# Delta rule by chunks: a group's heads in two halves of the partitions, with the scan's products alternating between the halves of the array

## Chip, cores and metric

The kernel runs on one core of one Trainium2 chip. The metric is the device time of one execution in microseconds. Before the change three timed runs took 1833.44, 1835.93 and 1836.46 us, with a median of 1835.93.

## What is computed

The reference is one transformer block for 256 tokens of width 2048 in f32: modulation of the input by a vector c, a token mixer with two branches (attention in a window with sinks, and a gated delta rule), and a mixture of 32 experts of which each token uses two. The change touches the delta rule alone. It has 8 heads of dimension 128, and the 256 tokens are cut into 4 chunks of 64:

```python
def gated_delta_rule(q, k, v, g, beta):
    ...
    cum = jnp.cumsum(g, axis=-1)                  # inside each chunk
    a_mat = jnp.where(strict, beta[..., :, None] * kk * decay_incl, 0.0)
    t_mat = lax.linalg.triangular_solve(a_mat + eye, ...)
    u = t_mat @ (v * beta[..., None])
    w = t_mat @ (k * (beta * jnp.exp(cum))[..., None])
    qk = jnp.einsum('bhncd,bhnjd->bhncj', q, k) * decay_incl
    ...
    def step(state, xs):
        u_c, w_c, qk_c, qd_c, kd_c, dec_c = xs
        v_new = u_c - w_c @ state
        o_c = qd_c @ state + qk_c @ v_new
        state = dec_c[..., None, None] * state + jnp.swapaxes(kd_c, -1, -2) @ v_new
        return state, o_c
```

Ahead of it stand a causal convolution of width 4 over q, k and v and a SiLU; behind it a norm over each head and a gate.

## The kernel before

The weights stream through TensorE once. The input projection is cut into blocks of 128 output columns. A block comes as a tile of 1 MB; each half of it is split into a high and a low part (`split`, L272: a cast wh on ScalarE at L275, a difference wl on VectorE at L276), and 24 matmuls of 128x256 take a half (`mm3`, L279 to L282, into tiles named ws, wq, pp). These matmuls are called the stream here. In between, VectorE works off the modulation of the second half of the block (`ada_steps`, L211: products with w_ada at L220).

The branches are Python generators, called chains. `run` (L345) goes through the list of jobs (one job is one half of a block), and between the quarters of each job it lets the chain take steps: `per` steps a job, where a step is what the generator does up to its next `yield`, and counts 1 unless the yield gives another number. What is left of a chain after the last job is issued at once. The stages around the change are these:

- L775: `gates`, the attention and a SiLU as the chain, 1.66 steps a job, with the first 12 blocks of q, k and v as the stream;
- L777: `gdn(0)`, heads 0 to 3, 1.55 steps a job, with the second 12 blocks;
- L823: `gdn(1)`, heads 4 to 7, 0.85 steps a job, with gate and output projections;
- L840: `out_b`, which turns the outputs o back (L831) and multiplies them with the gate.

A scheduler then fixes each engine's queue when the program is built. It can pull a few stream matmuls of the next run in among the last steps of a chain. On the chip each queue runs in that order.

In `gdn` (L459) the partitions hold tokens: 128 of them, that is two chunks, c=0 in partitions 0 to 63 and c=1 in 64 to 127. A unit u = 4t + h is head h in the tokens of tile t. After norms (L484 to L502), decays (L510 to L520) and the products pk and pq (L530, L531), a solve over six levels (L555 to L573) inverts the matrix of each chunk and head. Its products (`each`, L539 to L544) are 64x64 blocks, and with c innermost they alternate between rows and columns 0 to 63 of the array and 64 to 127. Each level has a step py for t=0, one for t=1, then a step prr (with ptt) for t=0 and one for t=1.

The scan (L579 to L618) goes through the chunks ci = 0 to 3 with the state St (128 x 4 heads x 128). Chunk ci lies in one half r of the partitions, and so all four heads' products of a group use the same half:

- ks and qs (L588, L592): keys and queries times the state, 128 rows of the array and 64 columns, both followed by VectorE on 64 x 512 (L589, L590, L593);
- vn (L600): the solved matrix times the corrected values, 64 rows and 64 columns, then a copy on ScalarE (L601);
- ds (L606): keys times new values, 64 rows and 128 columns, then decay on GpSimd (L608) and addition into St on VectorE (L609, L611);
- po (L614): 64 rows and 64 columns, then addition into o (L616, L618).

All of these go to PSUM tiles from one pool of five (`pg`, L141). In `conv_todo` (L444) ScalarE writes a scaled copy of a block to its place in G0 (L452), and VectorE adds three shifted ones in place (L454).

Of the kernel before, what the change touches and what calls it, by code (L numbers as in the profile page):

```python
# [16 lines left out]
P = 128  # L17
# [49 lines left out]
def tile_block(ctx: ExitStack, tc: tile.TileContext, A: dict, out: bass.AP, dbg=None, upto=99):  # L67
# [306 lines left out]
    beta = gd.tile([P, NT, GH], F32, name="beta")  # L374
    cum = gd.tile([P, NT, GH], F32, name="cum")
    ecum = gd.tile([P, NT, GH], F32, name="ecum")
    kdw = gd.tile([P, NT, GH], F32, name="kdw")
    dec = gd.tile([P, 2 * NT, GH], F32, name="dec")

    def gates():  # L380
# [55 lines left out]
        SC.activation(kdw, kdw, AF.Exp)  # L436

# [5 lines left out]

    def conv_todo(gi):  # L444
        g0s[gi] = r2.tile([P, 16, S], F32, tag=f"X{2 - gi}", name=f"G0{gi}")

        def use(m, ps):
            mi = 12 * gi + m
            y = g0s[gi][:, m, :]
            raw = gd.tile([P, S], F32, tag="cy", name=f"cy{mi}", bufs=2)  # L450
            SC.copy(raw, ps)
            SC.activation(y, ps, AF.Copy, scale=conv[:, mi, 3:4])  # L452
            for sft in (1, 2, 3):
                V.scalar_tensor_tensor(y[:, sft:], raw[:, :S - sft], conv[:, mi, 3 - sft:4 - sft], y[:, sft:],  # L454
                                       op0=MUL, op1=ADD)

        return [(20 + 12 * gi + m, lambda ps, m=m: use(m, ps)) for m in range(12)]

    def gdn(gi):  # L459
        h0 = gi * HG  # L460
        g0 = g0s[gi]
        qk, vT = g0[:, 0:8, :], g0[:, 8:12, :]
        kd = g0[:, 12:16, :].rearrange("p h s -> p (h s)").rearrange("p (t h d) -> p t h d", t=NT, h=HG)
        g1 = r1.tile([P, 1024 + 7 * 512], F32, tag="G1", name=f"G1{gi}")
        vt = g1[:, 0:1024].rearrange("p (t h d) -> p t h d", t=NT, h=HG)
# [11 lines left out]
        nn = gd.tile([P, 2, NT, HG], F32, tag="nn", name=f"nn{gi}")  # L477
        rn = gd.tile([P, 2, NT, HG], F32, tag="rn", name=f"rn{gi}", bufs=2)
        scr = gd.tile([P, P], F32, tag="scr", name=f"scr{gi}")
        for t in range(NT):  # L480
            for j in range(2):
                p = pg(f"nt{gi}{t}{j}")
                for h in range(HG):
                    T.transpose(p[:, h * P:(h + 1) * P], qk[:, 4 * j + h, t * P:(t + 1) * P], ident)  # L484
                for h in range(HG):
                    SC.activation(scr, p[:, h * P:(h + 1) * P], AF.Square, accum_out=nn[:, j, t, h:h + 1])
                if j:
                    V.tensor_copy(kd[:, t], p.rearrange("p (h d) -> p h d", h=HG))
            yield
        SC.activation(nn, nn, AF.Sqrt, bias=epsr)  # L490
        V.reciprocal(rn, nn)
        wj = gd.tile([P, NT, HG], F32, tag="wj", name=f"wj{gi}")
        wk = gd.tile([P, NT, HG], F32, tag="wk", name=f"wk{gi}")
        V.tensor_tensor(wj, rn[:, 1], rn[:, 1], op=MUL)
        V.tensor_tensor(wj, wj, beta[:, :, h0:h0 + HG], op=MUL)
        V.tensor_tensor(wk, wj, kdw[:, :, h0:h0 + HG], op=MUL)
        for t in range(NT):
            G.tensor_tensor(kd[:, t], kd[:, t], wk[:, t, :].unsqueeze(2).to_broadcast([P, HG, P]), op=MUL)
            p = pg(f"vv{gi}{t}")
            for h in range(HG):  # L500
                T.transpose(p[:, h * P:(h + 1) * P], vT[:, h, t * P:(t + 1) * P], ident)
            V.tensor_tensor(vt[:, t], p.rearrange("p (h d) -> p h d", h=HG),  # L502
                            nn[:, 1, t, :].unsqueeze(2).to_broadcast([P, HG, P]), op=MUL)
        yield
        cg = gd.tile([P, NT, HG], F32, tag="cg", name=f"cg{gi}")
        V.tensor_copy(cg, cum[:, :, h0:h0 + HG])
        cgu = cg.rearrange("p t h -> p (t h)").unsqueeze(2).to_broadcast([P, U, 64])
        wju = wj.rearrange("p t h -> p (t h)").unsqueeze(2).to_broadcast([P, U, 64])
# [15 lines left out]
        for t in range(NT):  # L524
            for h in range(HG):
                u = t * HG + h
                for c in range(2):
                    cs = slice(t * P + 64 * c, t * P + 64 * c + 64)
                    r = slice(64 * c, 64 * c + 64)
                    T.matmul(u3(pk)[r, u, :], qk[:, 4 + h, cs], qk[:, 4 + h, cs], start=True, stop=True)  # L530
                    T.matmul(u3(pq)[r, u, :], qk[:, 4 + h, cs], qk[:, h, cs], start=True, stop=True)  # L531
# [23 lines left out]
        for l in range(6):  # L555
            for t in range(NT):
                py = pg(f"py{gi}{l}{t}")[:, :256]
                each(py, BT, (lambda u: M("id64")) if l == 0 else (lambda u: u3(Tm)[:, u, :]), t)
                V.tensor_tensor(h3(half(Y, t)), h3(py), hb(lev[:, l, :]), op=MUL)
                yield  # L560
            for t in range(NT):
                prr = pg(f"prr{gi}{l}{t}")[:, :256]
                each(prr, Y, (lambda u: M("id64")) if l == 0 else (lambda u: u3(Rm)[:, u, :]), t)
                if l == 0:
                    G.tensor_tensor(h3(half(Tm, t)), hb(M("id64")), h3(half(Y, t)), op=SUB)
                    V.tensor_tensor(h3(half(Rm, t)), hb(M("id64")), h3(prr), op=SUB)
                else:
                    if l < 5:
                        pt = pg(f"ptt{gi}{l}{t}")[:, :256]
                        each(pt, Rm, lambda u: u3(Y)[:, u, :], t)  # L570
                        V.tensor_tensor(half(Tm, t), half(Tm, t), pt, op=SUB)
                    V.tensor_tensor(half(Rm, t), half(Rm, t), prr, op=SUB)
                yield  # L573

        f = lambda ap: ap.rearrange("p (h d) -> p h d", h=HG)
        X, Vn, St = f(b5[0]), f(b5[1]), f(b5[5])
        o = gd.tile([P, NT, HG, P], F32, tag="o", name=f"o{gi}", bufs=2)
        o_t[gi] = o
        for ci in range(2 * NT):  # L579
            t, c = ci // 2, ci % 2  # L580
            r = slice(64 * c, 64 * c + 64)
            cs = slice(t * P + 64 * c, t * P + 64 * c + 64)
            eb = ecum[r, t, h0:h0 + HG].unsqueeze(2).to_broadcast([64, HG, P])
            if ci:
                p1 = f(pg(f"ks{gi}{ci}"))
                p3 = f(pg(f"qs{gi}{ci}"))
                for h in range(HG):
                    T.matmul(p1[r, h, :], qk[:, 4 + h, cs], St[:, h, :], start=True, stop=True)  # L588
                V.tensor_tensor(X[r], p1[r], eb, op=MUL)  # L589
                V.tensor_tensor(X[r], vt[r, t], X[r], op=SUB)  # L590
                for h in range(HG):
                    T.matmul(p3[r, h, :], qk[:, h, cs], St[:, h, :], start=True, stop=True)  # L592
                V.tensor_tensor(o[r, t], p3[r], eb, op=MUL)  # L593
                xs = X[r]
                yield
            else:
                xs = vt[r, t]
            p2_ = f(pg(f"vn{gi}{ci}"))
            for h in range(HG):
                T.matmul(p2_[r, h, :], u3(Rm)[r, t * HG + h, :], xs[:, h, :], start=True, stop=True)  # L600
            SC.copy(Vn[r], p2_[r])  # L601
            yield
            if ci < 2 * NT - 1:
                p4 = f(pg(f"ds{gi}{ci}"))
                for h in range(HG):
# [6 lines left out]
            p5 = f(pg(f"po{gi}{ci}"))  # L612
            for h in range(HG):
                T.matmul(p5[r, h, :], u3(qkT)[r, t * HG + h, :], Vn[r, h, :], start=True, stop=True)  # L614
            if ci:
                V.tensor_tensor(o[r, t], o[r, t], p5[r], op=ADD)  # L616
            else:
                V.tensor_copy(o[r, t], p5[r])  # L618
            yield
        ssq = gd.tile([P, NT, HG], F32, tag="ssq", name=f"ssq{gi}")  # L620
        rq = gd.tile([P, NT, HG], F32, tag="rq", name=f"rq{gi}")
        for t in range(NT):
            for h in range(HG):
                SC.activation(scr, o[:, t, h, :], AF.Square, accum_out=ssq[:, t, h:h + 1])
# [6 lines left out]
        for t in range(NT):  # L631
            G.tensor_tensor(o[:, t], o[:, t], ssq[:, t, :].unsqueeze(2).to_broadcast([P, HG, P]), op=MUL)
# [192 lines left out]
    def out_b():  # L825
        oo = r2.tile([P, 2, 8, S], F32R, tag="X1", name="oB")
        oh[1], ol[1] = oo[:, 0], oo[:, 1]
        for j in range(8):
            p = pg(f"ot{j}")
            for t in range(NT):  # L830
                T.transpose(p[:, t * P:(t + 1) * P], o_t[j // HG][:, t, j % HG, :], ident)  # L831
            V.scalar_tensor_tensor(szT[:, j, :], p[:, :S], SM("nw"), szT[:, j, :], op0=MUL, op1=MUL)
            hilo(oh[1][:, j, :], ol[1][:, j, :], szT[:, j, :])
            yield
# [694 lines left out]
```

## Time and profile before

| | us |
|---|---|
| median of three timed runs | 1835.93 |
| the profiled execution | 1836.7 |
| its span, first to last instruction | 1834.7 |
| TensorE busy in it | 1742.0 |
| VectorE busy | 906.3 |
| ScalarE busy | 516.5 |
| GpSimd busy | 42.1 |

The mean granted TensorE clock is 0.987 of full speed. In a row of the profile stand line, engine, operation, output and inputs with their shapes, the count, then busy time in us and the mean of one in ns, then the idle time of the engine ahead of it and what ended it. A shape such as 64*64 ahead of an operand is the part of the array that a matmul uses, rows by columns. PE is TensorE, PEld its weight loads, DVE VectorE, ACT ScalarE, POOL GpSimd, SP the queue that issues transfers. Ends of matmuls are modelled, so that distances are better read from start to start.

### The profile page before, as it was taken

How to read it: one execution, taken by the hardware profiler on the slowest of the kernel's cores; microseconds unless marked ns; L12 is line 12 of the kernel's file. 1: busy time of each engine (PE TensorE's matmuls, PEld its weight loads, DVE VectorE, ACT ScalarE, POOL GpSimd, SP SyncE). 2: the span in 40 equal slices, each digit the busy share in tenths (PEclk: the TensorE clock that was granted, in tenths of full speed). 3: DMA queues.
4: the chain of work that ended last, by engine and by line, in shares of the span. 5: the costliest groups of instructions: out<-in, count | busy, mean ns of one | idle time of the engine just before them, and what ended most of it. 6: DMA issues, size and time to landing. Idle time of an engine off the chain costs nothing. (4 is left out here: it accounts for less than half of the span.)

```text
span 1834.7 us, 27454 instructions
## 1 busy us (share of the span) xinstructions
PE 1742.0 (95%) x11514; PEld 1122.4 (61%) x11514; DVE 906.3 (49%) x1447; ACT 516.5 (28%) x956; POOL 42.1 (2%) x47
## 2 busy tenths in 40 slices
PE   5999999999999999998899999999999999999995
PEld 3778988898999999986444443444434444344341
DVE  3355898788878878668233222332223312232135
ACT  3333699336323444434211100111101110011101
POOL 1000000102000000000000000000000000000000
PEclk8999999999999999999999999999999999999998
DMA  8888566455877578878799999999999999999995
GB/s 356 320 320 312 211 245 225 174 207 200 300 266 269 205 284 325 345 303 354 319 383 420 420 420 421 420 421 420 421 420 420 420 421 420 420 420 421 401 422 232
DMA packets 87287, 628.58 MB, mean 343 GB/s; under 512 B 9828, under 2 KB 9828, under 8 KB 11252
## 3 DMA queue, kind: packets, MB, share of 16 engines
q1 hardware_dynamic: 86832, 626.43, 85.6%
q8 instruction: 92, 1.51, 0.3%
q10 hardware_dynamic: 328, 0.36, 0.1%
q14 instruction: 35, 0.29, 0.0%
HBM read 624.65 MB, written 2.10 MB: 342 GB/s over the span
## 5 line engine op out<-in xcount | busy, mean ns | idle before, releaser
L275 ACT CAST wh<-w 128x1024 fp32r<-128x1024 f32 x216 | 225.9, 1049 | 319.0 <-PE ws L281 114.1
L276 DVE TENSOR_TENSOR wl<-w,wh 128x1024 fp32r<-128x1024 f32 x216 | 264.8, 1226 | 81.0 <-PE mx L281 22.8
L1187 PE MATMUL pg<-w,XT 128*64 128x512 f32 x1024 | 277.9, 598 | 5.0 <-DMA w<-in_w_gu 2.8
L1187 PE MATMUL pu<-w,XT 128*64 128x512 f32 x1024 | 274.6, 592 | 0.0
L280 PE MATMUL ws<-uh,wh 128*128 128x256 f32 x896 | 261.2, 292 | 1.1 <-ACT wh L275 1.1
L282 PE MATMUL ws<-uh,wl 128*128 128x256 f32 x896 | 254.5, 284 | 4.4 <-DVE wl L276 3.9
L281 PE MATMUL ws<-ul,wh 128*128 128x256 f32 x896 | 253.7, 283 | 0.0
L1225 PE MATMUL pd<-w,hT 128*64 128x512 f32 x1016 | 234.1, 599 | 0.8 <-DVE hT L1202 0.8
L1194 DVE TENSOR_TENSOR hs<-hs,pu 128x512 f32<-128x512 f32 x16 | 11.0, 688 | 429.3 <-PE pu L1187 429.3
L280 PEld LDWEIGHTS ws<-uh,wh 128*128 128x128 f32 x896 | 169.8, 190 | 11.6 <-issue 7.5
L282 PEld LDWEIGHTS ws<-uh,wl 128*128 128x128 f32 x896 | 170.1, 190 | 8.6 <-DVE wl L276 7.1
L281 PEld LDWEIGHTS ws<-ul,wh 128*128 128x128 f32 x896 | 170.1, 190 | 0.5 <-issue 0.5
L220 DVE SCALAR_TENSOR_TENSOR acc<-w,csil,acc 128x1024 f32<-128x1024 f32 x128 | 164.3, 1300 | 10.6 <-DMA w<-in_w_ada 10.3
L1187 PEld LDWEIGHTS pu<-w,XT 128*64 128x64 f32 x1024 | 77.6, 137 | 146.2 <-issue 146.2
L1187 PEld LDWEIGHTS pg<-w,XT 128*64 128x64 f32 x1024 | 72.3, 136 | 135.5 <-issue 111.8
L1166 PEld LDWEIGHTS xg<-G,xh 128*128 128x128 f32 x1024 | 118.9, 191 | 41.2 <-issue 25.8
L1225 PEld LDWEIGHTS pd<-w,hT 128*64 128x64 f32 x1016 | 66.5, 136 | 124.0 <-issue 109.6
L1166 PE MATMUL xg<-G,xh 128*128 128x128 f32 x1024 | 130.5, 281 | 6.8 <-DVE x L1242 3.5
L1193 ACT ACTIVATE hs<-pg 128x512 f32<-128x512 f32 x16 | 9.6, 598 | 439.1 <-PE pg L1187 439.1
L370 ACT CAST dh<-pd 128x512 fp32r<-128x512 f32 x64 | 37.5, 586 | 281.3 <-DVE pd L1228 160.8
L1228 DVE SCALAR_TENSOR_TENSOR pd<-pd,wsl,g2b 128x512 f32<-128x512 f32 x64 | 48.5, 758 | 104.0 <-PE pd L1225 104.0
L280 PE MATMUL wq<-uh,wh 128*128 128x256 f32 x320 | 93.7, 296 | 5.1 <-ACT uh L176 2.7
(365 smaller groups left out, 2298.0 us busy)
## 6 DMA issues: line engine op xcount, KB each, us to landing
w<-in_w_gu SPq DMA_DIRECT2D x256, 1024.0 KB, 19.8
w<-in_w_dn SPq DMA_DIRECT2D x127, 1024.0 KB, 19.8
w<-in_w_ada SPq DMA_DIRECT2D x64, 1024.0 KB, 5.0
w<-in_w_in SPq DMA_DIRECT2D x56, 1024.0 KB, 5.0
w<-in_w_a SPq DMA_DIRECT2D x28, 1024.0 KB, 6.3
w<-in_w_kq SPq DMA_DIRECT2D x20, 1024.0 KB, 6.4
w<-in_w_pab SPq DMA_DIRECT2D x16, 1024.0 KB, 5.3
w<-in_w_out SPq DMA_DIRECT2D x16, 1024.0 KB, 6.0
```

Of the source, the lines that this page charges most:

```text
L220: V.scalar_tensor_tensor(acc[:, hc], w[:, hc], csil[:, k:k + 1], acc[:, hc], op0=MUL, op1=ADD)
L275: SC.copy(h, w)
L276: V.tensor_tensor(lo, w, h.bitcast(F32), op=SUB)
L280: T.matmul(p, a[0], b[0], start=first, stop=False)
L281: T.matmul(p, a[0], b[1], start=False, stop=False)
L282: T.matmul(p, a[1], b[0], start=False, stop=last)
L370: SC.copy(h, src)
L1166: T.matmul(p[:, k * P:(k + 1) * P], xh[t][:, (4 * kq + k) * P:(4 * kq + k + 1) * P], Gs[t].bitcast(F32), start=(t == 0), stop=(t == NT - 1))
L1187: T.matmul(dst[64 * e:64 * e + 64, :], XT[:, k, 64 * e:64 * e + 64], we[:, e * 1024 + hv * 512:e * 1024 + hv * 512 + 512], start=(k == 0), ...
L1194: V.tensor_tensor(hs, hs, pup, op=MUL)
L1225: T.matmul(pd[64 * e:64 * e + 64, :], hT[:, f, 64 * e:64 * e + 64], we[:, (2 * (f % 2) + e) * 512:(2 * (f % 2) + e + 1) * 512], start=(f = ...
L1228: V.scalar_tensor_tensor(pd, pd, ws, g2b[:, cs], op0=MUL, op1=MUL)
```

## The change

The partitions of the delta rule no longer hold two chunks of a head, but one chunk of two heads. With a = 0 or 1 for the half of the partitions and e = 0 or 1 for the place within it, head e + 2a of a group stands in half a; a unit is u = 2 ci + e. So:

- the four products of each group in the scan alternate between the halves (the list `heads`), and the VectorE and ScalarE operations behind them are on 128 x 256 instead of 64 x 512. The two halves of ds go to two PSUM tiles, and are added into St in two operations. This makes one more PSUM tile per chunk out of the same pool of five;
- in the solve, both t are issued in one step, which counts 2;
- q, k and v are stored by place, chunk, half and token (`units`). The convolution therefore builds its sum in a tile of its own (cs, two of them, by turns), and its last addition writes to G0 in four pieces of 64;
- the gates beta, cum, ecum and kdw stand in one tile, gates4. A new last step of `gates` swaps the halves with two products (sw) and copies them to gc4, by chunk and head; each `gdn` then takes four small copies from there in place of one (cg);
- `out_b` turns two heads at once: four products into a tile, instead of two.

The diff, cut to its core:

```diff
@@ gates
+        yield
+        p = pg("sw")[:, :8 * GH].rearrange("p (q h) -> p q h", h=GH)
+        gq = gates4.rearrange("p q t h -> p (q t) h")
+        for a in range(2):
+            T.matmul(p[64 * a:64 * a + 64], ident[:, 64 - 64 * a:128 - 64 * a], gq, start=True, stop=True)
+        for a in range(2):
+            r = slice(64 * a, 64 * a + 64)
+            for c, src in ((a, gq), (1 - a, p)):
+                V.tensor_copy(gc4[r, :, c], src[r].rearrange("p q (g a e) -> p q a g e", g=2, a=2)[:, :, a])
...
@@ conv_todo
+        return g0[:, 4 * j:4 * j + 4, :].rearrange("p h s -> p (h s)").rearrange("p (e c a i) -> p e c a i", e=2, c=4, a=2)
...
-            SC.activation(y, ps, AF.Copy, scale=conv[:, mi, 3:4])
-            for sft in (1, 2, 3):
-                V.scalar_tensor_tensor(y[:, sft:], raw[:, :S - sft], conv[:, mi, 3 - sft:4 - sft], y[:, sft:],
+            SC.activation(sm[:, 1:], ps[:, :S - 1], AF.Copy, scale=conv[:, mi, 2:3])
+            for sft in (2, 3):
+                V.scalar_tensor_tensor(sm[:, sft:], raw[:, :S - sft], conv[:, mi, 3 - sft:4 - sft], sm[:, sft:],
                                        op0=MUL, op1=ADD)
+            V.scalar_tensor_tensor(y, raw.rearrange("p (c i) -> p c i", c=4), conv[:, mi, 3:4],
+                                   sm.rearrange("p (c i) -> p c i", c=4), op0=MUL, op1=ADD)
...
@@ gdn, solve
                 each(py, BT, (lambda u: M("id64")) if l == 0 else (lambda u: u3(Tm)[:, u, :]), t)
                 V.tensor_tensor(h3(half(Y, t)), h3(py), hb(lev[:, l, :]), op=MUL)
-                yield
+            yield 2.0
...
-                yield
+            yield 2.0
...
@@ gdn, scan
+        heads = [(e + 2 * a, slice(64 * a, 64 * a + 64), e) for e in range(2) for a in range(2)]
...
-                for h in range(HG):
-                    T.matmul(p1[r, h, :], qk[:, 4 + h, cs], St[:, h, :], start=True, stop=True)
-                V.tensor_tensor(X[r], p1[r], eb, op=MUL)
-                V.tensor_tensor(X[r], vt[r, t], X[r], op=SUB)
+                for h, r, e in heads:
+                    T.matmul(p1[r, e, :], ks[:, e, ci, h // 2], St[:, h, :], start=True, stop=True)
+                V.tensor_tensor(X, p1, eb, op=MUL)
+                V.tensor_tensor(X, vt[:, us], X, op=SUB)
...
-            for h in range(HG):
-                T.matmul(p2_[r, h, :], u3(Rm)[r, t * HG + h, :], xs[:, h, :], start=True, stop=True)
-            SC.copy(Vn[r], p2_[r])
+            for h, r, e in heads:
+                T.matmul(p2_[r, e, :], u3(Rm)[r, 2 * ci + e, :], xs[r, e, :], start=True, stop=True)
+            SC.copy(Vn, p2_)
             yield
             if ci < 2 * NT - 1:
-                p4 = f(pg(f"ds{gi}{ci}"))
-                for h in range(HG):
-                    T.matmul(p4[:, h, :], kd[r, t, h, :], Vn[r, h, :], start=True, stop=True)
+                p4 = [f2(pg(f"ds{gi}{ci}{a}")) for a in range(2)]
+                for h, r, e in heads:
+                    T.matmul(p4[h // 2][:, e, :], kd[r, 2 * ci + e, :], Vn[r, e, :], start=True, stop=True)
                 if ci:
                     G.tensor_tensor(St, St, dec[:, ci, h0:h0 + HG].unsqueeze(2).to_broadcast([P, HG, P]), op=MUL)
-                    V.tensor_tensor(St, St, p4, op=ADD)
-                else:
-                    V.tensor_copy(St, p4)
...
+                for a in range(2):
+                    if ci:
+                        V.tensor_tensor(St[:, 2 * a:2 * a + 2], St[:, 2 * a:2 * a + 2], p4[a], op=ADD)
+                    else:
+                        V.tensor_copy(St[:, 2 * a:2 * a + 2], p4[a])
```

qs and po change as ks and vn do. The transposes and the pk and pq products keep their number and shapes, with other columns of G0.

More of the change, by code (lines that the diff above doesn't have):

```diff
@@ L371, in hilo, with by_chunk @@
         V.tensor_tensor(lo, src, h.bitcast(F32), op=SUB)
[L374 to L377, printed above, removed]
+    gates4 = gd.tile([P, 4, NT, GH], F32, name="gates4")
+    beta, cum, ecum, kdw = [gates4[:, q] for q in range(4)]
+    gc4 = gd.tile([P, 4 * NT, 2, 2, 2], F32, name="gc4")
+    def by_chunk(q, gi):
+        return gc4[:, NT * q:NT * q + NT, :, gi].rearrange("p t c e -> p (t c) e")
     dec = gd.tile([P, 2 * NT, GH], F32, name="dec")
@@ L442, in tile_block, with units @@
     o_t = [None, None]
+    def units(g0, j):
+        return g0[:, 4 * j:4 * j + 4, :].rearrange("p h s -> p (h s)").rearrange("p (e c a i) -> p e c a i", e=2, c=4, a=2)
+    cys = [gd.tile([P, S], F32, name=f"cs{j}") for j in range(2)]
+    for cy in cys:
+        G.memset(cy[:, 0:1], 0.0)
     def conv_todo(gi):
@@ L523, in gdn @@
         pq = pg(f"pq{gi}")
[L524 to L531, printed above, removed]
+        for u in range(U):
+            q_, k_ = qs[:, u % 2, u // 2], ks[:, u % 2, u // 2]
+            for a in range(2):
+                r = slice(64 * a, 64 * a + 64)
+                T.matmul(u3(pk)[r, u, :], k_[:, a], k_[:, a], start=True, stop=True)
+                T.matmul(u3(pq)[r, u, :], k_[:, a], q_[:, a], start=True, stop=True)
         yield
@@ L578, in gdn @@
         o_t[gi] = o
+        heads = [(e + 2 * a, slice(64 * a, 64 * a + 64), e) for e in range(2) for a in range(2)]
         for ci in range(2 * NT):
[L580 to L583, printed above, removed]
+            us = slice(2 * ci, 2 * ci + 2)
+            eb = eg_[:, us].unsqueeze(2).to_broadcast([P, 2, P])
             if ci:
[L585 to L589, printed above, removed]
-                V.tensor_tensor(X[r], vt[r, t], X[r], op=SUB)
[L591 to L594, printed above, removed]
+                p1 = f2(pg(f"ks{gi}{ci}"))
+                p3 = f2(pg(f"qs{gi}{ci}"))
+                for h, r, e in heads:
[3 more added lines that the diff above has]
+                for h, r, e in heads:
+                    T.matmul(p3[r, e, :], qs[:, e, ci, h // 2], St[:, h, :], start=True, stop=True)
+                V.tensor_tensor(o[:, us], p3, eb, op=MUL)
+                xs = X
@@ L612, in gdn @@
-            p5 = f(pg(f"po{gi}{ci}"))
-            for h in range(HG):
-                T.matmul(p5[r, h, :], u3(qkT)[r, t * HG + h, :], Vn[r, h, :], start=True, stop=True)
+                for a in range(2):
+                    if ci:
+                        V.tensor_tensor(St[:, 2 * a:2 * a + 2], St[:, 2 * a:2 * a + 2], p4[a], op=ADD)
+                    else:
+                        V.tensor_copy(St[:, 2 * a:2 * a + 2], p4[a])
+            p5 = f2(pg(f"po{gi}{ci}"))
+            for h, r, e in heads:
+                T.matmul(p5[r, e, :], u3(qkT)[r, 2 * ci + e, :], Vn[r, e, :], start=True, stop=True)
@@ L625, in gdn @@
+        rq = gd.tile([P, U], F32, tag="rq", name=f"rq{gi}")
+        for u in range(U):
+            SC.activation(scr, o[:, u, :], AF.Square, accum_out=ssq[:, u:u + 1])
         V.tensor_scalar(rq, rn[:, 0], 128 ** -0.5, None, op0=MUL)
```

90 lines of the change are left out of this document (49 added, 41 removed).

## Prediction

> **What bounds the kernel now.** I read the page first, then the busy time by stage, then who waited for whom on the way to the end of the delta rule, then TensorE's timeline.
>
> ```profile
> span 1834.7 us, 27454 instructions
> PE 1742.0 (95%) x11514; PEld 1122.4 (61%) x11514; DVE 906.3 (49%) x1447; ACT 516.5 (28%) x956; POOL 42.1 (2%) x47
> ```
>
> TensorE is busy for 95% of the span, but that is an average. The stages show where the change lies (columns: from and to in us, length, busy us of PE, PEld, DVE, ACT and POOL with counts, granted clock, DMA share, GB/s):
>
> ```profile
> 200.00:302.00 102.00, 95.65 (x762) 87.20 (x760) 92.40 (x167) 90.81 (x235) 0.92 (x3) 1.00 0.63 230
> 302.00:430.00 128.00, 124.02 (x1362) 112.39 (x1361) 100.50 (x145) 54.24 (x108) 13.09 (x10) 0.97 0.52 188
> 430.00:614.00 184.00, 180.97 (x1856) 170.15 (x1854) 149.91 (x176) 72.18 (x125) 17.80 (x12) 1.00 0.73 270
> 640.00:760.00 120.00, 119.47 (x995) 117.39 (x994) 96.33 (x113) 52.89 (x71) 1.81 (x1) 1.00 0.83 306
> ...
> 1000.00:1400.00 400.00, 390.82 (x1944) 167.23 (x1942) 107.67 (x214) 41.10 (x90) 0.00 (x0) 1.00 1.01 420
> ```
>
> The first row is gates and attention, the next two are gdn(0) and gdn(1). In all of them TensorE works through one queue in which projection matmuls (the stream: ws, pp) alternate with steps of the delta rule. It stands still for 4.0 of 128 us in gdn(0) and 3.0 of 184 in gdn(1), and VectorE is at 79% and 81%. So there a microsecond less of TensorE instructions is a microsecond less of time, as long as the other engines keep up. The last row is the expert stage: DMA share 1.01 at 420 GB/s. It is bound by transfers, but its loads start when the earlier stages have freed their buffers, and from 640 to 760 us TensorE is busy for 119.5 of 120 us; what is saved before 614 us therefore moves the whole expert stage forward, at one to one.
>
> Who TensorE waited for, 200 to 640 us (total, times, longest):
>
> ```profile
> PE py L544 <- DVE G L535: 5.1, 2, 4.0
> PE pa L708 <- DVE attP L699: 2.0, 1, 2.0
> ```
>
> These few waits are what a shorter queue could lengthen.
>
> **What a detour costs.** One f32 product is two passes in the trace. A group of four scan products, all on one half of the array (vn, 64*64), stands between stream matmuls like this:
>
> ```profile
> 394.01 0.28 PE L281 MATMUL ws<-ul,wh 128*128 128x256 f32 x1
> 394.13 0.28 PE L282 MATMUL ws<-uh,wl 128*128 128x256 f32 x1
> 394.33 1.08 PE L600 MATMUL vn<-G 64*64 64x128 f32 x8
> 395.35 0.39 PE L280 MATMUL ws<-uh,wh 128*128 128x256 f32 x1
> 395.57 0.28 PE L281 MATMUL ws<-ul,wh 128*128 128x256 f32 x1
> ```
>
> Stream matmuls start 0.12 us apart. From 394.13 to the second one behind the group at 395.57 are 1.44 us; two stream steps would be 0.24, so the detour costs 1.20. Now two detours of the solve, whose products already alternate between (0,0) and (64,64), one of 16 passes and one of 32:
>
> ```profile
> 336.21 0.28 PE L282 MATMUL ws<-uh,wl 128*128 128x256 f32 x1
> 336.42 0.68 PE L544 MATMUL py<-G 64*64 64x64 f32 x16
> ...
> 337.26 0.28 PE L281 MATMUL ws<-ul,wh 128*128 128x256 f32 x1
> ...
> 342.07 0.27 PE L282 MATMUL ws<-uh,wl 128*128 128x256 f32 x1
> 342.28 0.68 PE L544 MATMUL prr<-G 64*64 64x64 f32 x16
> 342.79 0.63 PE L544 MATMUL ptt<-G 64*64 64x64 f32 x16
> ...
> 343.58 0.28 PE L281 MATMUL ws<-ul,wh 128*128 128x256 f32 x1
> ```
>
> They cost 1.05-0.24=0.81 and 1.51-0.24=1.27. The difference, 0.46, is 16 passes (0.029 each); the rest of the first, 0.35, is paid once per detour. Taken off vn: (1.20-0.35)/8=0.106 per pass of 128 columns, so 0.053 for one of 64 alone. The solve's passes take 0.029: alternating halves ran 1.84 times as fast. The same holds for the two other shapes: pk and pq (128*64, columns alternating) and attention's s (64*128, rows alternating, two banks):
>
> ```profile
> 313.86 0.28 PE L282 MATMUL ws<-uh,wl 128*128 128x256 f32 x1
> 314.07 0.34 PE L530 MATMUL pk<-G 128*64 128x64 f32 x4
> ...
> 316.35 0.28 PE L281 MATMUL ws<-ul,wh 128*128 128x256 f32 x1
> ...
> 216.34 1.13 PE L660 MATMUL s<-a 64*128 64x256 f32 x8
> 217.40 0.38 PE L282 MATMUL ws<-uh,wl 128*128 128x256 f32 x1
> ```
>
> pk and pq: 2.49-0.24-0.35=1.90 for 64 passes, 0.030 each, 1.8 times. s: 8 passes that alone would be 0.212 each (1.70) are done in 1.06, at least 1.6 times.
>
> **The change, part by part.** (1) Scan. There are 8 vn, 8 po, 6 ks, 6 qs and 6 ds groups, 34, each 8 passes of 128 columns, 0.85 us. At 1.84 times each is 0.46: 0.39 saved, 34 x 0.39 = -13.3. Ends: 1.6 times gives -10.9, twice gives -14.5.
>
> [...]
>
> (2) Solve. Both halves t are now issued in one step. The first place on PE where gdn(0) issues prr and ptt (the stream's ws around them), before:
>
> ```order
> L281 MATMUL ws_3456<-ul,wh 128x256
> L282 MATMUL ws_3456<-uh,wl 128x256
> L544 MATMUL prr_3500<-G_3030 64x64 x8
> L544 MATMUL ptt_3509<-G_3030 64x64 x8
> L280 MATMUL ws_3456<-uh,wh 128x256
> ```
>
> and after (t=0 and t=1 in a row):
>
> ```order
> L282 MATMUL ws_3481<-uh,wl 128x256
> L573 MATMUL prr_3515<-G_3039 64x64 x8
> L573 MATMUL ptt_3524<-G_3039 64x64 x8
> L573 MATMUL prr_3535<-G_3039 64x64 x8
> L573 MATMUL ptt_3544<-G_3039 64x64 x8
> L280 MATMUL ws_3481<-uh,wh 128x256
> ```
>
> Two detours became one. Counted over the order, the six levels make 23 and 24 detours before and 12 and 12 after: 23 x 0.35 = -8.0. (3) The cover thereby shrinks: 30 to 36 stream matmuls (3.5 to 4.2 us) between two steps in gdn(0) instead of about 5 us, while VectorE gets two tiles' work at once. In its queue may stand
>
> ```profile
> L276 DVE TENSOR_TENSOR wl<-w,wh 128x1024 fp32r<-128x1024 f32 x216 | 264.8, 1226 | 81.0 <-PE mx L281 22.8
> L220 DVE SCALAR_TENSOR_TENSOR acc<-w,csil,acc 128x1024 f32<-128x1024 f32 x128 | 164.3, 1300 | 10.6 <-DMA w<-in_w_ada 10.3
> L572 DVE TENSOR_TENSOR G<-G,prr 128x256 f32<-128x256 f32 x20 | 8.3, 414 | 0.1
> L589 DVE TENSOR_TENSOR G<-ks,ecum 64x512 f32<-64x512 f32 x6 | 4.1, 691 | 3.6 <-PE ks L588 3.5
> ```
>
> one of the first (1.23), one of the second (1.30) and two of the third: 3.4 us, just covered; four of the third and one of the first: 2.9. I take +1.5 (0 to 12).
>
> (4) VectorE in the scan: operations on 64x512 (0.69) become 128x256 (0.41), 18 of them with PSUM operands, saving 5 us of VectorE; ds is added in two parts, +0.14 x 6; ten more small copies come in all, none dearer than a 128x256 operation (0.41); the convolution keeps three additions per column block, the last now written with gaps (0.41 again, or twice that at worst: 12 blocks in a stage, +5 us). Who waits for VectorE here is TensorE, for wl and for the solve's tiles. In gdn(0) the worst of all this is (100.5-2.5+0.4+2+5)/118=89%, under the 91% of the attention stage, where TensorE waited little. So 0; what it costs when that cover goes is rival B.
>
> (5) End of gdn(0)'s scan on PE, before (ds, po: products with the state; ks, qs: the next chunk's first):
>
> ```order
> L614 MATMUL po_4350<-G_3030 64x128 x4
> L282 MATMUL ws_4410<-uh,wl 128x256
> L280 MATMUL ws_4410<-uh,wh 128x256
> L281 MATMUL ws_4410<-ul,wh 128x256
> L588 MATMUL ks_4356<-G_3030,G_1443 64x128 x4
> L592 MATMUL qs_4357<-G_3030,G_1443 64x128 x4
> ```
>
> and after:
>
> ```order
> L646 MATMUL po_4371<-G_3039 64x128 x4
> L618 MATMUL ks_4377<-G_3039,G_1445 64x128
> L622 MATMUL qs_4378<-G_3039,G_1445 64x128
> L282 MATMUL ws_4431<-uh,wl 128x256
> L280 MATMUL ws_4431<-uh,wh 128x256
> L281 MATMUL ws_4431<-ul,wh 128x256
> L618 MATMUL ks_4377<-G_3039,G_1445 64x128 x3
> L622 MATMUL qs_4378<-G_3039,G_1445 64x128 x3
> ```
>
> ks now stands right behind po, with only po's 0.5 us to cover the first state addition (0.41 and the way there), and the next vn has 9 stream matmuls (1.1 us) of cover instead of 23. +1.5 (0 to 3), and +0.35 for the split detour.
>
> (6) Gates and attention: the product sw with four copies, one more step. On PE, sw is a detour, +0.45. It stands 20 stream matmuls behind cl, and vt and s behind it, where vt followed cl at once; attention starts 2.4 us later in its stage, in which ACT and DVE are at 89% and 91% and the gaps in the convolution's write could take half of DVE's free 10 us. Who waits is TensorE, for the last units' turned probabilities (pa, above). +1.5 (-2 to +4).
>
> (7) Start of gdn(1) on POOL. The two operations with wk took
>
> ```profile
> 453.23 3.02 POOL L498 TENSOR_TENSOR G<-G,wk 128x512 f32<-128x512 f32 x2
> ```
>
> and stood behind the decay's mask (L519) and its factor wj, ahead of the strict mask (L534):
>
> ```order
> L519 TENSOR_TENSOR G_4442<-G_4442,cmx 128x512
> L520 TENSOR_TENSOR G_4442<-G_4442,wj_4602 128x512
> L498 TENSOR_TENSOR G_3006<-G_3006,wk_4603 128x512 x2
> L534 TENSOR_TENSOR G_4442<-G_4442,cmx 128x512
> L565 TENSOR_TENSOR G_4442<-cmx,G_4442 128x256 x2
> ```
>
> and after:
>
> ```order
> L532 TENSOR_TENSOR G_3015<-G_3015,wk_4632 128x512 x2
> L550 TENSOR_TENSOR G_4463<-G_4463,cmx 128x512
> L551 TENSOR_TENSOR G_4463<-G_4463,wj_4631 128x512
> L563 TENSOR_TENSOR G_4463<-G_4463,cmx 128x512
> L594 TENSOR_TENSOR G_4463<-cmx,G_4463 128x256 x2
> ```
>
> Now wk comes first and the first mask is queued behind it, so the chain starts once wk is there, up to 3.0 us later; the first py waits at its end, with 60 stream matmuls of cover instead of 54. +1.0 (0 to 3).
>
> (8) The one long wait:
>
> ```profile
> 326.06 1.97 PE L544 MATMUL py<-cmx,G 64*64 64x64 f32 x32 [3.98 <-DVE G L535]
> 326.00:332.00 6.00, 5.94 (x61) 5.51 (x62) 3.43 (x6) 1.69 (x3) 1.45 (x2) 0.51 0.45 161
> ```
>
> It gets 55 stream matmuls of cover instead of 48: -0.8. After it the clock was 0.51 for 6 us, which cost 2.9. With a wait of some 3.2 us the drop may stay away; I count nothing for it and keep 2.9 for the low end.
>
> [...]
>
> The loads' order is the same on SP. The tail's ot (8 detours of two become 4 of four) I count as nothing.
>
> Sum: -13.3-8.0+1.5+1.5+0.35+0.45+1.5+1.0-0.8 = -15.8. The profiled execution took 1836.7 us, 0.8 above the median of the three timed runs (1835.9): 1820.1 against that median. A change under 0.2% (3.7 us) can hardly be told from none here.
>
> **Rivals.** A, the halves do not run at once. vn and po write both halves into one bank, ks and qs share their rows; without these 28 groups 10.9 us are missing: 1831. Against it: py is of vn's form, in one bank, and ran at 1.84. For it: no row shows 128-column passes of these groups, or their order of operands. Chance 0.10.
>
> [...]
>
> B, the covers in (3) are too short: ten joints in gdn(0), each late by one wl (1.2 us), 12 in place of 1.5: 1830.6. It decides once VectorE's queue behind a step is longer than 3.5 us, against 3.4 by the rows. Chance 0.14.
>
> C, slower: attention. If it slides so that TensorE waits about 3 us for each of its four units, and the clock halves after each as in (8), each costs 5.9: +23.6 in place of 1.5, 1842. It passes zero change when three of the four come about. Against it: waits of up to 2.0 us stand there now and the clock in that stage is 1.00. Chance 0.07.
>
> The forecast has 0.69. **Range:** the low end has twofold halves (1.2), the clock drop gone (2.9), and the losses of (3), (5), (6) and (7) nearly nil (5): 1811. The high end takes in A and B: 1831. Faster by over 0.2%: the forecast, nearly all of A, over half of B, 0.86; same 0.07; slower 0.07.
>
> **What would show it.** In the changed trace a vn detour should cost about 0.8 us in place of 1.20, ds and po together 0.8 less than now, prr and ptt twice about 2.2; gdn(0) should shrink by about 8 us, gdn(1) by about 10, and everything from 640 us on only shift. Passes of vn 0.1 us apart would mean A; waits of py and prr for VectorE, B; new waits before 302 us with a clock under 0.9, C. I am wrong if the two delta-rule stages shrink as forecast and the expert stage does not start earlier.

## Result, and the profile after

The changed kernel takes 1821.51 us (median of 4 runs, 1817.45 to 1823.21) against 1835.28 (median of 4) for the kernel before: ratio 0.9922, 95% interval 0.9905 to 0.9939. The profiled execution took 1820.14 us, against 1836.7 before.

The same views as in the prediction. The page's first lines, then the stages of the changed kernel (columns as there):

```profile
span 1818.2 us, 27495 instructions
PE 1724.2 (95%) x11518; PEld 1108.4 (61%) x11518; DVE 899.9 (49%) x1463; ACT 516.7 (28%) x957; POOL 45.2 (2%) x49
```

```profile
200.00:302.00 102.00, 92.79 (x733) 84.08 (x731) 91.97 (x173) 87.11 (x227) 0.91 (x3) 0.99 0.62 226
302.00:430.00 128.00, 124.27 (x1431) 114.22 (x1432) 105.99 (x161) 62.98 (x135) 15.49 (x10) 0.96 0.57 210
430.00:614.00 184.00, 179.74 (x1912) 170.55 (x1911) 151.50 (x196) 76.04 (x127) 21.53 (x14) 0.98 0.74 270
```

TensorE's busy time fell by 17.8 us and the span by 16.5. But the clock is a little lower than it was in each of these windows (0.99, 0.96 and 0.98 against 1.00, 0.97 and 1.00). TensorE's waits for py are longer than before in all, and those for pb are new (200 to 640 us, changed kernel):

```profile
PE py L573 <- DVE G L564: 6.2, 2, 3.3
PE pb L749 <- ACT PT L743: 3.5, 2, 3.3
PE ws L282 <- DVE wl L276: 1.6, 3, 0.8
PE pa L740 <- DVE attP L731: 1.4, 2, 0.8
PE pa L740 <- ACT attP L730: 1.2, 1, 1.2
```

So there are losses beside the gains. Places in the program at which the same number of stream matmuls has gone by show where. TensorE's timeline of the kernel before, at the first pk, the first vn and the last po of gdn(1):

```profile
447.94 0.34 PE L530 MATMUL pk<-G 128*64 128x64 f32 x4
...
564.45 1.08 PE L600 MATMUL vn<-G 64*64 64x128 f32 x8
...
613.52 1.08 PE L614 MATMUL po<-G 64*64 64x128 f32 x8
```

And of the changed kernel, with the first pk of gdn(0) and the first vn detour ahead of them:

```profile
318.75 0.34 PE L559 MATMUL pk<-G 128*64 128x64 f32 x4
...
394.83 0.28 PE L282 MATMUL ws<-uh,wl 128*128 128x256 f32 x1
395.04 0.65 PE L630 MATMUL vn<-G 64*64 64x128 f32 x8
395.63 0.38 PE L280 MATMUL ws<-uh,wh 128*128 128x256 f32 x1
395.85 0.28 PE L281 MATMUL ws<-ul,wh 128*128 128x256 f32 x1
...
441.72 0.34 PE L559 MATMUL pk<-G 128*64 128x64 f32 x4
...
557.98 0.65 PE L630 MATMUL vn<-G 64*64 64x128 f32 x8
...
599.82 0.65 PE L646 MATMUL po<-G 64*64 64x128 f32 x8
```

| stretch | before | after | change |
|---|---|---|---|
| start to first pk of gdn(0) | 314.07 | 318.75 | +4.7 |
| to its first vn (start and solve) | 80.26 | 76.29 | -4.0 |
| to the first pk of gdn(1) (scan) | 53.61 | 46.68 | -6.9 |
| to its first vn | 116.51 | 116.26 | -0.25 |
| to its last po (scan) | 49.07 | 41.84 | -7.2 |
| to the end | 1221.2 | 1218.4 | -2.8 |

The column adds up to -16.5, the change of the span; in the last two rows three stream matmuls (0.4 us) have changed sides. What follows the last po has moved ahead as a whole, and 2.8 us are gained in it in this pair of executions. Two rows are not what a shorter queue gives: the first, where 4.7 us are lost before the delta rule has begun, and the fourth, where the solve of gdn(1) should have gained 4 and gained nothing. The experiments go after both, and after the reason for the scan's gain.

Each column is one profiled execution, and such a row varies. In the changed kernel and the five runs below whose edits act on the scan, the solve or the masks, TensorE and ScalarE have the same work in the same order up to the first pk, and it came at 317.31 to 320.44 us. The last row took 1219.3 to 1222.4 us in the eight runs below that start from the changed kernel, and 1220.6 to 1225.1 in the three that start from the kernel before. So the 4.7 us of the first row are more than chance, though their size is uncertain by some 1.5; the 2.8 us of the last row may be chance.

### The profile page after: what moved, and what is told of

It is laid out like the page before. It is cut to its first block, busy times and chain, and to the rows that moved or that the text cites. A ratio compares the mean times of both kernels' runs of the same rounds, so it can differ in the third digit from the quotient of the medians.

```text
span 1818.2 us, 27495 instructions
## 1 busy us (share of the span) xinstructions
PE 1724.2 (95%) x11518; PEld 1108.4 (61%) x11518; DVE 899.9 (49%) x1463; ACT 516.7 (28%) x957; POOL 45.2 (2%) x49
```

## Experiments

Each ran against the kernel before on the same chip; that took 1836.83, 1836.52 and 1835.62 us (medians) in the three sets of runs, so differences in per cent go by the ratios. The changed kernel's own ratio is 0.9922 [0.9905, 0.9939].

**Does the order within a group matter?** In the scan, both heads of one half first:

```diff
-        heads = [(e + 2 * a, slice(64 * a, 64 * a + 64), e) for e in range(2) for a in range(2)]
+        heads = [(e + 2 * a, slice(64 * a, 64 * a + 64), e) for a in range(2) for e in range(2)]
```

> The changed kernel with one edit: the list of heads in the scan goes through both heads of half 0 first and then both of half 1, so that in each group of four products the halves no longer alternate; shapes, instructions, stream and solve stay. My theory (the scan's gain is that passes on different halves of the array run at once): inside one half the passes follow each other at 0.106 us again and only the joint between the halves overlaps, 7 of 8 pass times; a vn detour goes from 0.78 back to about 1.10 us, 34 groups lose 0.32 to 0.37 each, +11 to +12.6, so about 1833 us against 1821.5. Rival (the gain came from the 128 x 256 operations behind the products and from shorter waits, not from the array): the time stays within 2 us of 1821.5 and vn stays at 0.78.

1823.12 us, ratio 0.9928 [0.9903, 0.9952]: no loss. The first vn group on TensorE:

```profile
395.62 0.66 PE L630 MATMUL vn<-G 64*64 64x128 f32 x8
```

Its eight passes take 0.66 us, as with alternation (0.65 above) and not as with one half (1.08 before). My theory as stated fell, and the rival had the time right; but the group still ran as two halves at once do, so the rival's reason (no gain from the array) is not shown by it either. What remained was a third theory: each half works through its own products, and the order in the queue is free up to some depth. That was tried where groups are longer, in the solve's `each`, eight products with the four of one half first:

```diff
-            for h in range(HG):
+            for h, c in [(h, c) for c in range(2) for h in range(HG)]:
                 u = t * HG + h
-                for c in range(2):
+                if True:
```

> The changed kernel with the solve's products in blocks: in each group of eight products of 64x64 first the four of chunk half 0 and then the four of half 1, where they alternated before and after the change; the scan is as changed. In the run with the scan's two heads of a half in a row, passes still started in pairs, so the order inside a group of four products did not matter. Theory A (each half of the array works through its own queue, and the next products are issued ahead of the ones that run): also eight passes on end for a half cost nothing, py detours stay at 1.27 us and the time within 2 us of 1821.5. Theory B (one half can be ahead of the other by only some four passes): each of 64 groups loses about 0.2 us, +13, about 1834, and a py detour of two groups is 1.6 to 1.7. Theory C (alternation is needed here): 0.42 for each group, +27, about 1848.

1834.14 us, ratio 0.9990 [0.9978, 1.0003], 12.5 us (0.68%) more than the changed kernel: the size that theory B gave. A py step of two groups, in the changed kernel and in this one:

```profile
351.71 1.15 PE L573 MATMUL py<-G 64*64 64x64 f32 x32
```

```profile
340.96 1.54 PE L573 MATMUL py<-G 64*64 64x64 f32 x32
```

The same 32 passes take 0.39 us longer, and a detour of prr and ptt in four groups went from 2.20 to 2.81. That is 0.2 and 0.15 us a group, about 11 us for the 64 groups. So the gain does come from the two halves running at once (eight vn passes in 0.65 us, 1.08 on one half): with the same products in an order that puts eight passes of one half on end, part of it is gone. How far one half can be ahead of the other, by which theory B explained it, no row shows. Four passes on end for one half cost nothing, eight cost 0.15 to 0.2 us a group; what lies between was not tried.

**Fixed cost of a detour.** The solve's steps as they were, in both halves of a level:

```diff
                 V.tensor_tensor(h3(half(Y, t)), h3(py), hb(lev[:, l, :]), op=MUL)
-            yield 2.0
+                yield
...
```

> The changed kernel with the solve's steps as they were: a yield of 1 behind each t, so 23 more detours. My theory (each detour costs 0.35 us beside its passes, and the shorter covers of the merged steps cost next to nothing): +8, about 1829 us, with the py and prr detours at 0.80 and 1.27 again. Rival (merging gives back in waits for VectorE what it saves in detours): +4 or less, 1825 or under.

1830.47 us, ratio 0.9969 [0.9953, 0.9986]: 0.47%, 8.6 us, more than the changed kernel. The detours are back at 0.80 (py) and 1.27 (prr with ptt), so the 0.35 us for each of 23 holds; TensorE waits for VectorE there about as long as in the changed kernel (6.6 us for py and a wl, against 6.2 for py), so merging gave nothing back. That the time agrees so well is luck in part: in the profile the stretches of the two solves are 6.4 us longer, and 1.7 us stand ahead of the first pk, where the two kernels do the same.

**Where the attention's 4.7 us went.** First guess, the swap of the gates moved behind the attention:

```diff
         SC.activation(kdw, kdw, AF.Exp)
         yield
+
+    def swap():
         p = pg("sw")[:, :8 * GH].rearrange("p (q h) -> p q h", h=GH)
...
+        yield
...
-    ch = seq(gates(), attn_v(), attn(), z_silu())
+    ch = seq(gates(), attn_v(), attn(), swap(), z_silu())
```

> The changed kernel with the step that swaps the halves of the gates (sw and its four copies) moved behind the attention, so that attention starts at the same stream matmul as before the change. In the changed kernel the first pk stands at 318.75 us against 314.07 before, 4.7 later. My theory (those 4.7 us come from attention starting 20 stream matmuls later, which ends in waits for ScalarE and a lowered clock): the first pk comes at 314 to 315 and the time falls by 3.5 to 5, to about 1817. Rival (they come from the convolution's other operations on VectorE and ScalarE): pk stays at 318 and the time within 1.5 us of 1821.5.

1824.19 us, ratio 0.9930 [0.9905, 0.9955], with the first pk not earlier but at 323.96 us. This missed, and the order says why it was no earlier: the edit left the added `yield` at the end of the gates, so every step of the attention was still issued one step later. That left two suspects, the added step and the convolution, and each was put alone into the kernel before the change: its convolution built in the two small tiles, and an empty step at the end of its gates.

```diff
-            SC.activation(y, ps, AF.Copy, scale=conv[:, mi, 3:4])
-            for sft in (1, 2, 3):
-                V.scalar_tensor_tensor(y[:, sft:], raw[:, :S - sft], conv[:, mi, 3 - sft:4 - sft], y[:, sft:],
+            sm = cys[m % 2]
+            SC.activation(sm[:, 1:], ps[:, :S - 1], AF.Copy, scale=conv[:, mi, 2:3])
+            for sft in (2, 3):
+                V.scalar_tensor_tensor(sm[:, sft:], raw[:, :S - sft], conv[:, mi, 3 - sft:4 - sft], sm[:, sft:],
                                        op0=MUL, op1=ADD)
+            V.scalar_tensor_tensor(y, raw, conv[:, mi, 3:4], sm, op0=MUL, op1=ADD)
```

```diff
         SC.activation(kdw, kdw, AF.Exp)
+        yield
```

> The kernel before the change with one part of the change alone: the convolution builds its sum in two small tiles by turns and its last addition writes the block; the layout and the steps stay, and the attention's steps stand at the same stream matmuls as in the kernel before. The question is why the first pk came 4.7 us later in the changed kernel. Theory A (the convolution's two shared tiles tie ScalarE and VectorE together): the first pk comes at 317 us or later against 314.07, and the time is 3 to 5 over 1835.9. Theory B (the convolution has no part in it): pk at 313 to 315.5, the time within 2 us of 1835.9.

> The kernel before the change with one more step in the gates' chain (an empty yield behind the last gate), so that all steps of the attention are issued one step later; with that its products stand at the same stream matmuls as in the run with the swap moved behind the attention, which kept that step and came late all the same. Theory A (the added step alone makes the attention's end late): the first pk comes at 317 us or later against 314.07, and the time is 3 to 7 over 1835.9. Theory B (the step has no part in it): pk at 313 to 315.5, the time within 2 us of 1835.9.

The convolution alone: 1835.40 us, ratio 0.9994 [0.9984, 1.0003], first pk at 314.56. (It writes the block in one piece, not in four; in the changed kernel the writing in pieces took 0.47 us, as the other additions did, at 336.25 us.) The empty step alone: 1841.74 us, ratio 1.0036 [1.0025, 1.0047], first pk at 321.20. It is the step. The run with the swap moved has the same longest wait for the copy PT as this one, 3.8 us; why it is longer there than with sw ahead of the attention (3.25) is not shown. Late in that stage, in the kernel with the empty step (TensorE's timeline, the wait in brackets):

```profile
298.56 0.87 PE L718 MATMUL pb<-PT,a 128*64 128x256 f32 x8 [3.79 <-ACT PT L712]
```

and in the changed kernel, with its windows:

```profile
298.05 0.87 PE L749 MATMUL pb<-PT,a 128*64 128x256 f32 x8 [3.25 <-ACT PT L743]
```

```profile
296.00:302.00 6.00, 1.86 (x11) 0.97 (x11) 5.50 (x9) 5.89 (x12) 0.00 (x0) 0.79 0.45 156
302.00:308.00 6.00, 5.83 (x35) 5.15 (x36) 2.17 (x3) 4.99 (x11) 0.00 (x0) 0.64 0.67 270
```

The same wait stands in both: the last units of the attention stand together at the end of the stage, where ScalarE has work for 5.9 of 6 us, TensorE waits over 3 us for the copy PT, and its clock is low behind it. ScalarE was as full there before the change (5.97 us from 296 to 302); it is the later steps that reach it too late. A faster chain was tried too:

```diff
-PER = (1.66, 1.55, 0.85, 2.0)
+PER = (1.75, 1.55, 0.85, 2.0)
```

> The changed kernel with 1.75 steps of the chain a job in place of 1.66 while the gates and the attention run, so that the last pa stands at stream matmul 1538 and not 1566, 3.3 us earlier by the stream. Theory A (the attention's end is late because its steps are issued too late after the added step): the waits for pb and pa before the first pk (6.1 us in the changed kernel) shrink by half or more, the first pk comes 3 us or more earlier, and the time falls to about 1818. Theory B (the chain is held up by the queues of ScalarE and VectorE, in whatever place its steps are issued): TensorE waits as long in other places, and the time stays within 2 us of 1821.5.

1821.05 us, ratio 0.9900 [0.9877, 0.9924]: not told apart from the changed kernel. The waits of pa and pb fell from 6.3 to 2.0 us, the first pk came 2.4 earlier (1.0 before the earliest of the six above), and then the stream waited 3.7 us for one wl in gdn(0), with the clock at 0.74 and 0.69 from 326 to 338 us. What was gained was given back at once.

**The first py.** It stands 23 stream matmuls later in gdn(0) and 24 in gdn(1):

```diff
         V.tensor_tensor(BT, pk, decb, op=MUL)
         yield
+        yield (3.0, 1.0)[gi]
...
-            yield 2.0
+            yield (1.73, 1.91)[gi]
```

> The changed kernel with the first py step 23 or 24 stream matmuls later in both halves of the delta rule, and the later steps of the solve closer together, so that the scan starts where it did. In the changed kernel TensorE waits 3.3 and 2.9 us there, and the granted clock is near 0.5 for about 5 us behind each wait. My theory (wait and lowered clock are both lost time, and the steps behind have room): 6.2 us of waits and 5 to 6 of clock go, 9 to 12 in all, to about 1811. Rival (the solve's chain through VectorE sets the pace, and 24 to 30 matmuls of cover are too few): the waits turn up again at the later py and prr, and the time stays at 1819 or above.

1818.57 us, ratio 0.9910 [0.9880, 0.9939]: close under the rival's bound of 1819 and far from 1811, though not in the way the rival gave. The wait did not come back at many later steps but at once, as waits for the stream's wl (1.24 us in gdn(0), 2.64 in gdn(1)) and for one prr (1.36): VectorE had no free time there (6.00 of 6 us busy in each window from 320 to 338). What holds VectorE up is in its own timeline, changed kernel, gdn(0):

```profile
322.28 1.28 DVE L529 TENSOR_TENSOR wk<-wj,kg 128x8 f32<-128x8 f32 x1
323.48 1.21 DVE L276 TENSOR_TENSOR wl<-w,wh 128x1024 fp32r<-128x1024 f32 x1
324.62 1.26 DVE L477 SCALAR_TENSOR_TENSOR cs<-cy,sml,cs 128x254 f32<-128x254 f32 x1
...
326.98 2.06 DVE L276 TENSOR_TENSOR wl<-w,wh 128x1024 fp32r<-128x1024 f32 x1
328.96 1.48 DVE L479 SCALAR_TENSOR_TENSOR G<-cy,sml,cs 128x256 f32<-128x256 f32 x1
```

and GpSimd's beside it:

```profile
321.16 2.37 POOL L550 TENSOR_TENSOR G<-G,cmx 128x512 f32<-128x512 f32 x1 [73.27 <-issue]
323.61 1.99 POOL L551 TENSOR_TENSOR G<-G,wj 128x512 f32<-128x512 f32 x1
325.56 2.40 POOL L532 TENSOR_TENSOR G<-G,wk 128x512 f32<-128x512 f32 x2
327.92 2.24 POOL L563 TENSOR_TENSOR G<-G,cmx 128x512 f32<-128x512 f32 x1
```

An operation on 128x8 takes 1.28 us, a wl 2.06, a convolution's addition 1.26 or 1.48. GpSimd's own times vary too: the mask of L550 takes 2.37 us here and 1.32 in gdn(1). With these five GpSimd operations on VectorE:

```diff
-            G.tensor_tensor(kd[:, us], kd[:, us], wk[:, us].unsqueeze(2).to_broadcast([P, 4, P]), op=MUL)
+            V.tensor_tensor(kd[:, us], kd[:, us], wk[:, us].unsqueeze(2).to_broadcast([P, 4, P]), op=MUL)
...
-        G.tensor_tensor(u3(decb), u3(dg), ub(M("incl")), op=MUL)
-        G.tensor_tensor(u3(decb), u3(decb), wju, op=MUL)
+        V.tensor_tensor(u3(decb), u3(dg), ub(M("incl")), op=MUL)
+        V.tensor_tensor(u3(decb), u3(decb), wju, op=MUL)
...
-        G.tensor_tensor(u3(decb), u3(decb), ub(M("strict")), op=MUL)
+        V.tensor_tensor(u3(decb), u3(decb), ub(M("strict")), op=MUL)
```

> The changed kernel with the masks, the factor wj and the factor wk of the delta rule's start on VectorE in place of GpSimd. In the changed kernel these five operations take 9.0 us of GpSimd ahead of the first py of gdn(0) (2.37, 1.99, 2.40 and 2.24 us), VectorE's operations beside them are stretched (a difference wl 2.06 us where 1.22 is its mean), and TensorE waits 3.3 us there and 2.9 in gdn(1), with a granted clock near 0.5 behind. My theory (GpSimd's chain, and what it does to VectorE, is what the first py waits for): on VectorE an operation is 0.69 us, the waits go but for a rest under 1 us, the clock stays, and the time falls by 8 to 12 us to about 1811. Rival (VectorE's own queue is what is late at this place, since it had no idle time from 321 to 339 us in the run with the later py either): the wait moves to wl or stays, and the time falls by less than 3.

```profile
321.71 0.16 DVE L529 TENSOR_TENSOR wk<-wj,kg 128x8 f32<-128x8 f32 x1
321.85 1.23 DVE L276 TENSOR_TENSOR wl<-w,wh 128x1024 fp32r<-128x1024 f32 x1
322.99 1.29 DVE L532 TENSOR_TENSOR G<-G,wk 128x512 f32<-128x512 f32 x2
324.19 0.69 DVE L551 TENSOR_TENSOR G<-G,wj 128x512 f32<-128x512 f32 x1
324.79 0.48 DVE L477 SCALAR_TENSOR_TENSOR cs<-cy,sml,cs 128x254 f32<-128x254 f32 x1
```

1812.10 us, ratio 0.9867 [0.9849, 0.9884], 0.55% or 10 us below the changed kernel: as my theory said. The operations are 0.16 and 0.48 again, the masks cost 0.6 to 0.7 each, and of 6.2 us of waits for py 0.2 are left. The run does not separate two causes, GpSimd's own chain (9.0 us for what takes VectorE some 3.4) and what it does to VectorE's queue: in gdn(0) of the changed kernel VectorE never stood still ahead of the first py, but in gdn(1) it waited 1.16 us for GpSimd's last mask itself. Of VectorE's operations ahead of the first py in gdn(0), those that are stretched beside GpSimd (1.28, 1.26, 2.06 and 1.48 us in the rows above) all read two tensors from SBUF; the product L562, which reads one of its two inputs from PSUM, took 0.68 beside GpSimd and 0.69 without it, and the wl that stayed at 1.21 started (323.48) ahead of GpSimd's next operation (323.61). What stretches them no run here shows.

Did the kernel before suffer as much from it? The same edit there:

> The kernel before the change with the masks and the factors wj and wk on VectorE, as in the last run of the changed kernel, which fell to 1812.1 us. Theory A (GpSimd's chain was as dear in the kernel before, where the first py waited 4.0 us in gdn(0) with 6 us of clock at 0.51 behind, and 1.1 in gdn(1)): those 5.1 us and 2.9 of clock go, -8, about 1828. Theory B (the changed kernel lost by it what the kernel before did not): -4 or less, 1832 or above.

1829.05 us, ratio 0.9961 [0.9949, 0.9974]: 7 us, nearer to theory A. With GpSimd out of the way in both, the change is worth 0.9867/0.9961=0.9906. In these two profiles both solves gain what they should: the second row of the table goes from 74.64 to 70.54 us and the fourth from 114.65 to 110.15.

**A version that beats both.** Masks on VectorE, and the swap behind the attention, this time without the added step. Beside the edits above:

```diff
         SC.activation(kdw, kdw, AF.Exp)
-        yield
+
+    def swap():
```

> The changed kernel with the masks on VectorE, and with the swap of the gates moved behind the attention without the added step, so that the attention's products stand at the stream matmuls of the kernel before. Theory A (the added step makes the attention late): the first pk comes at 314 to 315.5 us against 318.77 with the masks alone, and the time falls from 1812.1 to about 1808. Theory B (the convolution or something else does): pk stays at 317 or later and the time within 2 us of 1812.1.

1808.16 us, ratio 0.9851 [0.9835, 0.9868], first pk at 314.82. The two largest waits from 200 to 322 us are back at what the kernel before had (2.3 and 2.0):

```profile
PE ws L282 <- DVE wl L276: 2.2, 4, 0.9
PE pa L742 <- DVE attP L733: 2.1, 1, 2.1
```

It is 27.5 us (1.5%) under the kernel before the change and 13.4 under the changed one.

## Why the prediction was right, step by step

The forecast of 1820.1 met 1821.51, and -15.8 stood against -16.6 of the profiled executions (-13.8 of the medians). But several terms were off and cancelled: the mechanism of the gain was right, and that the sum came so close was luck in part.

- (1) Scan: -13.3 forecast at 1.84 times. The vn detour went from 1.20 to 0.78 (395.85-394.83-0.24), 0.42 a group; read in the same way, ds with po and ks with qs went from 2.29 and 2.08 to 1.42 and 1.21, 0.435 a group: twice as fast, 34 groups make about -14.7. The mechanism was right; alternation itself, by which I named it, is not needed in a group of four (0.66 us for vn without it, 0.65 with it). Rival A (a bank, or shared rows, keeps the halves apart) did not come: ks and qs share their rows, vn and po write both halves into one tile of the pool, and all gained about the same (0.435 a group for ks and qs, and for ds with po; 0.42 for vn). The detour of ks and qs, before (2.08) and after (1.21):

```profile
401.17 0.28 PE L282 MATMUL ws<-uh,wl 128*128 128x256 f32 x1
401.38 1.09 PE L588 MATMUL ks<-G,G 128*64 128x128 f32 x8
...
403.49 0.28 PE L281 MATMUL ws<-ul,wh 128*128 128x256 f32 x1
```

```profile
400.59 0.28 PE L282 MATMUL ws<-uh,wl 128*128 128x256 f32 x1
400.80 0.66 PE L618 MATMUL ks<-G,G 128*64 128x128 f32 x8
...
402.04 0.28 PE L281 MATMUL ws<-ul,wh 128*128 128x256 f32 x1
```

- (2) Solve: -8.0 forecast; by the detours (py 0.81+0.80 to 1.27, prr with ptt 2 x 1.27 to 2.21) it is 0.335 each, 7.7, and the run with the steps split, 8.6 us slower, agrees.
- (3) Shorter covers: +1.5 forecast, nothing found; no later py or prr waits. Rival B did not come.
- (5) The end of gdn(0)'s scan: of +1.85 about 0.9 came. vn waits 0.2 us for VectorE, the split detour cost 0.6.
- (6) Attention: +1.95 forecast, +4.7 measured, and this is rival C's mechanism on a smaller scale: one unit of four waited over 3 us with the clock at 0.64 behind it. I had priced the product sw at 0.45 and the later start, by the one added step with its 20 matmuls, at 1.5. The later start was mis-sized: an empty step alone cost the kernel before 7.1 us up to the first pk and 6.4 in time.
- (7) Start of gdn(1): +1.0 (0 to 3) forecast, about +3.8 measured (the 4.0 that the solve should gain there, less the 0.25 of the table). The first py there waits 2.87 us in place of 1.13, and the clock is low behind it:

```profile
454.05 1.23 PE L573 MATMUL py<-cmx,G 64*64 64x64 f32 x18 [2.87 <-DVE G L564]
```

```profile
450.00:456.00 6.00, 3.13 (x43) 2.84 (x42) 4.13 (x5) 1.05 (x1) 2.67 (x3) 0.76 0.58 239
456.00:462.00 6.00, 6.00 (x37) 6.00 (x37) 4.64 (x5) 2.71 (x3) 2.15 (x2) 0.67 0.51 177
```

  The low clock is bad luck in part: in the run with the solve in blocks the same py waited 2.86 us and the clock stayed:

```profile
459.43 1.51 PE L573 MATMUL py<-cmx,G 64*64 64x64 f32 x32 [2.86 <-DVE G L564]
```

```profile
458.00:464.00 6.00, 4.57 (x58) 4.53 (x59) 5.25 (x6) 1.55 (x3) 2.99 (x3) 1.00 0.16 55
```

  The step failed in its reason as well: I had the first mask wait on GpSimd's queue behind wk. The mask (446.84) waited for ScalarE's exponential, and that for a clamp (L548) that stood late in VectorE's queue and was itself stretched, beside wk on GpSimd, to 1.27 us (0.42 in the kernel before):

```profile
443.49 1.27 DVE L548 TENSOR_SCALAR G<-G 128x512 f32<-128x512 f32 x1
```

```profile
446.84 1.32 POOL L550 TENSOR_TENSOR G<-G,cmx 128x512 f32<-128x512 f32 x1 [1.18 <-ACT G L549]
```

  The clamp reads only one tensor, so reading two from SBUF does not account for its stretch; what does no run here shows.

- (8) The long wait of gdn(0) went from 3.98 to 3.34, -0.6 against -0.8; the low clock behind it stayed (0.58 from 332 to 338 us).
- What I counted as nothing: the tail from the last po on gained 2.8 us. In the kernel before, ot waited 1.42 us there and the clock was 0.84 from 620 to 628 us; in the changed kernel the longest wait is 0.7 and the clock 1.00. By the spread of that row (above) much of it may be chance: with the convolution alone in the kernel before, ot waited the same 1.42 us and the stream matmuls behind it stand 0.12 us apart (0.21 without that edit).

Measured: -14.7-7.7+0.9+4.7+3.8-0.6-2.8-1.0 (the stretch ahead of gdn(1)) = -17.4 against -16.5 of the span; 0.9 us are not assigned. (6) and (7) came out 5.5 dearer than forecast, and the other terms some 7 better, the tail, the covers and the scan above all.

## What to carry to other kernels

Where small products can use both halves of the array, put both into the same group (0.42 us a group of four here), and do not let one half have a long run of passes (four on end cost nothing here, eight 0.15 to 0.2 us a group); count a fixed cost, here 0.35 us, for each time the stream is left. A step added to a chain that feeds a tight queue moves everything behind it, so price the shift and not the step's own work. Before giving a wait more cover, look at whether the engine waited for is stretched by its neighbour or itself waits for it: here moving five GpSimd operations to VectorE was worth 10 us, and 23 matmuls more of cover nothing that could be told apart.

## What the runs showed of the hardware beyond this

- In a group of four products the order of the halves in the queue made no difference: four passes for half 0 and then four for half 1 took as long as alternating ones (a detour of 0.78). In a group of eight, eight and eight took 0.15 to 0.2 us longer a group.
- Beside GpSimd's operations on 128x512 some of VectorE's were stretched: wl from 1.22 to 2.06 us, a 128x8 operation from 0.16 to 1.28, while the product L562 kept its 0.68. GpSimd's own vary as much: a product of 128x512 with a mask took it 1.3 to 2.4 us, and VectorE 0.69.
- The clock did not go by the length of one wait alone. It was low behind waits of 3.98 us (0.51 in the kernel before, 0.53 with the convolution alone, both from 326 to 332 us), of 3.79 (0.65 from 302 to 308, the empty step), of 3.75 (0.69 from 332 to 338, the faster chain), and in the changed kernel of 3.34 (0.58) and 3.25 (0.64). Of shorter waits some had this and some not: 2.87 us had it and 2.86 did not (gdn(1), above); 2.03 us in the attention left 1.00 in the kernel before, and 2.01 with the masks on VectorE there stand beside 0.81 (290 to 296 us); 1.42 us ahead of ot left the stream matmuls behind it 0.12 us apart with the convolution alone, and in the kernel before the clock was low behind it:

```profile
625.17 0.54 PE L831 MATMUL ot<-cst,o 128*128 128x128 f32 x2 [1.42 <-POOL o L632]
```

```profile
626.00:628.00 2.00, 2.00 (x11) 2.00 (x11) 1.17 (x5) 1.94 (x4) 0.00 (x0) 0.50 0.94 381
```
